# Two FFN layers' entries and ends re-ordered, and the attention's 16-row value blocks padded to 128 rows

## The chip, the cores and the metric

The kernel runs on one core of a Trainium2 chip. The core has five engines that run at the same time and wait for one another only where data passes: TensorE (PE, matmuls), VectorE (DVE), ScalarE (ACT), GpSimd (POOL) and SyncE (SP, which issues the DMAs here). The metric is the device time of one execution in microseconds. Times of one execution are also given per engine from a profile.

## The reference, cut to what matters

Two layers over 1040 tokens (16 meta tokens ahead of 1024), width 1024. Each layer mixes attention and convolution, and then runs a SwiGLU FFN of width 2816:

```python
h = jnp.concatenate([meta, x], axis=1)                 # 16 + 1024 tokens
for l in range(2):
    hn = rmsnorm(h, norm1_g[l])
    q, k, v, u = jnp.split(hn @ w_in[l], ...)
    attn_out = diff_attention(q, k, v, lam, ...)       # a = p0 - lam*p1;  a @ v; causal, 4 heads
    conv_out = conformer_conv(u + b_glu[l], ...)       # width 31, layer norm, silu
    h = h + jnp.concatenate([attn_out, conv_out], axis=-1) @ w_out[l]
    hn = rmsnorm(h, norm2_g[l])
    gate, up = jnp.split(hn @ w_gate_up[l], 2, axis=-1)
    h = h + (jax.nn.silu(gate) * up) @ w_down[l]
return rmsnorm(h, final_g)[:, 16:]
```

All is float32. The kernel writes most products as three matmuls on a high and a low part of each operand (high*high, high*low, low*high).

## The kernel before

Activations lie transposed, channels on the 128 partitions and tokens along the free dimension. The 1040 tokens go in chunks `CH0` = 272, 384 and 384 (in the last layer `CH1`, 2 x 512, since the meta tokens are dropped). A layer has two phases, each with a tile pool of its own that is opened at its start and closed at its end.

**The mix phase.** For each head: `project_qk`, `project_v`, `attention`, woven together with the projections of the next head so that TensorE always has work. In `attention`, the 1040 keys are cut into nine blocks, the first of 16 (the meta tokens) and eight of 128. `turn` transposes the softmaxed rows of one query block into `aT` (128 keys by 128 queries) and, for the meta keys, into `aT0`, 16 rows by 128. `values` then sums over the key blocks in one PSUM tile: one matmul on 16 rows (`aT0` and `v0`) and then one on 128 rows for each further block (L482). A float32 matmul is two records in the trace.

After the heads come the convolution and the output projection `w_out`. Its attention half ("oa") runs beside the convolution's layer norm (`conv_norm`, which calls `rsqrt_bcast`), its convolution half ("oc") in a loop of its own at L861: eight output blocks n in the order `OCN` = 0, 4, 1, 5, 2, 6, 3, 7, each in three (last layer: two) chunks of 12 matmuls into a PSUM tile "pj", added into `acc[n]` (the tiles ST and p) by DVE. After each pair (k, k+4), `forms(k)` makes the seven operand forms of a Strassen-Winograd product ("a11", "s3", "s2", "a12", "s1", "a22", "s4") from `acc[k]` and `acc[k+4]`, each split into a high part (ACT) and a low part (DVE), and `squares` adds the squares of both for the norm ahead of the FFN.

**The FFN phase.** 22 blocks j of 128 FFN channels. For each, seven products, in the order `PRODS`, of 2 x 12 matmuls of 260 columns (last layer 12 of 512), on PSUM tiles "pj", "tr" and "sc". The weights of a product are combined and split by `prep`, called two products ahead through `ahead`. The product "s1" adds into the same PSUM tiles ("sc") as "s2"; between them ACT copies the tiles out (L943), and before the change "a12" stands between the two. The norm factor `rs` is worked out in block j = 0 at "s3" by `rsqrt_bcast`: matmuls with a column of ones (L179), a power on POOL (L186), a diagonal on DVE (L197), a broadcast by matmuls with ones (L198), a copy by ACT (L201). The finished blocks (`mids`, high and low part) are gathered in groups of `GROUPS` = 3, 3, 3, 3, 3, 3, 2, 2, and `down` multiplies a group by `w_down` and adds it into `acc`, at "s3" of the next block. Of the last group nothing is left to overlap with: in layer 0 it also makes the next layer's operands (L281 and L282) and squares, in layer 1 the final norm, chunk by chunk (`CHF`, 512, 256 and 256 tokens), with the output multiplications at L914 and the DMAs of the output.

**What sets the order.** A list scheduler sorts the instructions of each engine; waits between engines are semaphores. PSUM tags have 3 tiles ("pj"), 3 ("sc") and 2 ("tr"). The pool of big tiles "S" has 15, the pool "T" of temporaries 5, and the weight slots "w" 16.

## Time and profile before

| | us |
|---|---|
| median of three runs | 2444.1 (2441.98 to 2445.82) |
| the profiled execution, its own time | 2446.08 |
| its span, first to last instruction | 2444.3 |
| PE busy | 2369.1 (97%) |
| DVE busy | 1689.7 (69%) |
| ACT busy | 991.1 (41%) |
| POOL busy | 32.4 (1%) |

The span lies 1.8 us under the execution's own time. The mean granted clock of TensorE is 0.985. In the chain of work that ended last PE has 82%, DVE 12%, ACT 2%. The stages follow one another: mix of layer 0 to 467 us, its oc loop to 530, FFN of layer 0 to 1239, mix of layer 1 to about 1685, its oc loop to 1733, FFN of layer 1 to 2391.8, and the last group with the final norm to the end.

### The profile page before, as it was taken

What the parts mean: (1) busy time and instruction counts of PE and PEld (TensorE: products, weight loads), DVE (VectorE), ACT (ScalarE), POOL (GpSimd) and SP (SyncE); (2) the same over time, 40 slices, a digit from 0 to 9 for tenths busy, and PEclk for the clock granted to TensorE, in tenths of its full rate; (3) what the DMA queues carried; (4) which work ended last, traced back from release to release, by engine and by line L of the source; (5) the groups of instructions that cost most, each with busy time, mean ns of one, the idle gap of its engine ahead of it and who ended that gap; (6) DMA issues with size and microseconds to landing.
All of it is one profiled execution on the core that took longest, in us unless ns stands there. A gap on an engine that the chain in (4) does not pass through costs nothing.

```text
span 2444.3 us, 36772 instructions
## 1 busy us (share of the span) xinstructions
PE 2369.1 (97%) x14359; PEld 2154.2 (88%) x14359; DVE 1689.7 (69%) x3532; ACT 991.1 (41%) x2090; POOL 32.4 (1%) x21
## 2 busy tenths in 40 slices
PE   8999999989999999999999999999999999999996
PEld 7889999889999999999989999987788888888885
DVE  7676799776656656566776767997866556556566
ACT  5554462544224224233435545635533223223232
POOL 0000000000000000000000000000000000000000
PEclk9999999999999999999989999999999999999998
DMA  4322412101111111111144224221111111111112
GB/s 163 87 67 73 118 60 63 39 27 52 50 57 49 48 57 46 55 47 48 56 130 104 72 58 118 70 62 39 35 57 46 54 57 46 54 56 46 55 50 71
DMA packets 86764, 155.28 MB, mean 64 GB/s; under 512 B 10304, under 2 KB 37952, under 8 KB 86592
## 3 DMA queue, kind: packets, MB, share of 16 engines
q1 hardware_dynamic: 86592, 152.95, 21.6%
q8 instruction: 113, 1.85, 0.3%
q14 instruction: 59, 0.48, 0.1%
HBM read 114.64 MB, written 8.45 MB: 50 GB/s over the span
## 4 chain that ended last, share of the span: by engine, by line
PE 82%; DVE 12%; ACT 2%; issue 1%; POOL 1%; DMA 1%; SPq 1%; DVEq 0%; POOLq 0%; ACTq 0%
PE pj L271 25%; PE sc L856 15%; PE pj L856 10%; PE tr L856 10%; PE sc L271 9%; PE tr L482 4%; DVE S L569 3%; PE sc L434 2%; PE tr L471 1%; PE sc L435 1%; DVE S L158 1%; PE sc L198 1%; DVE T L285 1%; DVE S L285 1%; PE sc L179 1%
## 5 line engine op out<-in xcount | busy, mean ns | idle before, releaser
L271 PE MATMUL pj<-S,w 128*128 128x384 f32 (+2 forms) x1425 | 358.2, 357 | 16.9 <-DVE ST L285 13.4
L271 PE MATMUL pj<-hh,w 128*128 128x384 f32 (+1 forms) x1776 | 348.5, 331 | 3.1 <-ACT w L221 2.4
L277 ACT ACTIVATE w<-w 128x512 fp32r<-128x512 f32 x308 | 187.2, 627 | 309.8 <-DVE w L285 129.5
L271 PEld LDWEIGHTS pj<-hh,w 128*128 128x128 f32 x1776 | 290.6, 192 | 6.0 <-ACT w L221 2.7
L271 PEld LDWEIGHTS pj<-S,w 128*128 128x128 f32 x1425 | 254.6, 192 | 45.6 <-DVE ST L285 15.2
L856 PE MATMUL sc<-S,w 128*128 128x260 f32 (+1 forms) x1188 | 283.9, 320 | 0.0
L278 DVE TENSOR_TENSOR w<-w,w 128x512 fp32r<-128x512 f32 x308 | 210.1, 688 | 95.5 <-ACT w L277 35.9
L221 ACT ACTIVATE w<-w 128x512 fp32r<-128x512 f32 (+2 forms) x219 | 121.0, 553 | 284.3 <-DMA w<-in_w_down 265.1
L271 PE MATMUL sc<-m,w 128*128 128x384 f32 (+3 forms) x834 | 229.8, 349 | 0.0
L271 PE MATMUL pj<-m,w 128*128 128x384 f32 (+3 forms) x825 | 226.9, 349 | 0.0
L856 PEld LDWEIGHTS sc<-S,w 128*128 128x128 f32 x1188 | 196.3, 188 | 17.4
L222 DVE TENSOR_TENSOR w<-w,w 128x512 fp32r<-128x512 f32 (+2 forms) x219 | 130.9, 598 | 92.4 <-ACT w L221 47.0
L856 PE MATMUL sc<-hh,w 128*128 128x260 f32 (+1 forms) x594 | 189.8, 320 | 0.7 <-ACT sc L932 0.7
L856 PE MATMUL sc<-hl,w 128*128 128x260 f32 (+1 forms) x594 | 189.8, 319 | 0.0
L271 PE MATMUL pj<-hl,w 128*128 128x384 f32 (+1 forms) x888 | 175.9, 329 | 0.0
L271 PE MATMUL sc<-S,w 128*128 128x384 f32 (+3 forms) x474 | 164.6, 349 | 6.3 <-DVE ST L285 2.7
L271 PEld LDWEIGHTS sc<-m,w 128*128 128x128 f32 x834 | 150.7, 188 | 14.1
L271 PEld LDWEIGHTS pj<-m,w 128*128 128x128 f32 x825 | 148.7, 188 | 13.8
L856 PE MATMUL pj<-hh,w 128*128 128x260 f32 (+1 forms) x594 | 157.8, 320 | 1.1 <-DVE ST L285 1.1
L856 PE MATMUL tr<-S,w 128*128 128x260 f32 (+1 forms) x594 | 158.1, 320 | 0.1
L856 PE MATMUL tr<-hl,w 128*128 128x260 f32 (+1 forms) x594 | 158.1, 320 | 0.0
L856 PE MATMUL pj<-S,w 128*128 128x260 f32 (+1 forms) x594 | 157.8, 320 | 0.0
(199 smaller groups left out, 4495.8 us busy)
## 6 DMA issues: line engine op xcount, KB each, us to landing
w<-in_w_gu SPq DMA_DIRECT2D x176, 256.0 KB, 2.8
S<-ST SPq DMA_DIRECT2D x96, 260.0 KB, 5.3
w<-in_w_in SPq DMA_DIRECT2D x80, 256.0 KB, 3.2
w<-in_w_down SPq DMA_DIRECT2D x96, 192.0 KB, 2.4
w<-in_w_out SPq DMA_DIRECT2D x32, 256.0 KB, 2.7
S<-in_xT SPq DMA_DIRECT2D x8, 520.0 KB, 7.1
w<-in_w_down SPq DMA_DIRECT2D x32, 128.0 KB, 2.0
S<-in_tabs SPq DMA_DIRECT2D x4, 520.0 KB, 5.2
```

The source lines that it names most:

```text
L158: V.tensor_tensor(sqacc[:, c0:c1], sqacc[:, c0:c1], q[:, :c1 - c0], op=ALU.add)
L179: T_.matmul(pst[:b - a, i:i + 1], lhsT=t[:, a:b], rhs=ones[:, 0:1], start=(q == 0), stop=(q == len(sq) - 1))
L221: S.activation(hi, rw, AF.Copy)
L222: V.tensor_tensor(lo, rw, hi.bitcast(F32), op=ALU.subtract)
L271: T_.matmul(out, lhsT=w[k][wi], rhs=xs[k][xi][:, c0:c1], start=(q == 0 and k == 0), stop=(q == 2 and k == n - 1))
L277: S.activation(hi, src, AF.Copy)
L278: V.tensor_tensor(lo, src, hi.bitcast(F32), op=ALU.subtract)
L285: V.tensor_tensor(o, a, b, op=op)
L434: T_.matmul(pc[:sz, :n], lhsT=qs[:, qa:qb], rhs=kk[:, k0:k1], start=True, stop=False)
L482: T_.matmul(po[:sz, :P], lhsT=lh, rhs=rh, start=(j == 0), stop=(j == len(blocks) - 1))
L569: bg.append(lambda o=o: V.scalar_tensor_tensor(y[:, o:L], z[:, :L - o], cw(o), y[:, o:L], op0=ALU.mult, op1=ALU.add))
L856: T_.matmul(outs[c][:, :s1 - s0], lhsT=w[wi][:, k * P:(k + 1) * P], rhs=xc[q][k][xi][:, s0:s1], start=(first and p == 0 and k == 0), stop= ...
```

## The change

1. **Padding.** `make_pads`, at the opening of each mix phase, makes four tiles of 128 x 128 and sets them to zero on POOL. `v0` and `aT0` become the first 16 rows of such a tile (two of each, in turn), and the first matmul of `values` takes all 128 rows, 112 of them zero.
2. **The norm in two parts.** `rsqrt_bcast` becomes `rsqrt_cols` (sums and power) and `spread` (diagonal, broadcast, copy). In the FFN the first is called at "s2" of block 0 and the second at "s1"; `conv_norm` yields between them.
3. **Forms in pieces.** `forms(k)` becomes a generator of four pieces, whose high and low parts are interleaved across forms; a piece is taken after each chunk of the oc loop (`some(1)`). The oc chunks alternate between PSUM "pj" and "tr". The first weights of the FFN (`ahead(1)`) are prepared after the oc loop instead of ahead of it, and the squares of the last four output blocks are done inside block 0.
4. **Order of products.** "s1" now follows "s2" at once, ahead of "a12".
5. **Groups.** The groups are 3, 3, 3, 3, 3, 3, 4. The fourth block's result takes two S tiles. In the last group four outputs run over the first three blocks before the fourth is there (`early`). In layer 1 the closing of a chunk (norm and output) is written after the second output block of the next chunk (`owed`).

The core of the diff:

```diff
-GROUPS = ((3, 3, 3, 3, 3, 3, 2, 2), (3, 3, 3, 3, 3, 3, 2, 2))
+GROUPS = ((3, 3, 3, 3, 3, 3, 4), (3, 3, 3, 3, 3, 3, 4))
-PRODS = ("a11", "s3", "s2", "a12", "s1", "a22", "s4")
+PRODS = ("a11", "s3", "s2", "s1", "a12", "a22", "s4")
...
-                    plan.append((("dn", l, gi, n), (w_down[l, n, :, f0:f0 + gn, :], gn), end and n < 5))
+                    plan.append((("dn", l, gi, n), (w_down[l, n, :, f0:f0 + gn, :], gn), end and n >= 4))
...
+    def make_pads():
+        pads[:] = [[phase[1].tile([P, P], F32, tag=f"pad{i}{j}", name=nm("pad")) for j in range(2)]
+                   for i in range(2)]
+        for t in pads[0] + pads[1]:
+            G.memset(t, 0.0)
...
-        v0 = phase[1].tile([META, P], F32, tag="v0", name=nm("v0"), bufs=2)
+        v0 = padded(0)
...
-                S.activation(v0, px[:META, :P], AF.Copy, scale=rcol[:META, 0:1])
+                S.activation(v0[:META, :], px[:META, :P], AF.Copy, scale=rcol[:META, 0:1])
...
-                    aT0 = phase[1].tile([META, P], F32, tag="aT0", name=nm("aT0"), bufs=2)
-                    S.activation(aT0[:, :sz], ptg[:META, 384:384 + sz], AF.Copy)
+                    aT0 = padded(1)
+                    S.activation(aT0[:META, :sz], ptg[:META, 384:384 + sz], AF.Copy)
...
             S.activation(s4, y[:, b0:b1], AF.Copy, scale=e)
+            hi("a11")
+            tt(d, x[:, b0:b1], x[:, a0:a1], ALU.subtract)
             stt(s3, x[:, b0:b1], g, s4, ALU.subtract)
...
+            lo("a11")
+            hi("s3")
+            yield
             stt(s2, d, g, s4, ALU.subtract)
...
-        ahead(1)
...
+        no = 0
         for i, n in enumerate(OCN):
             w = fetch("oc", l, n)
             t = acc[n]
             for c0, c1 in chunks:
-                po = ps("pj")
+                po = ps(("pj", "tr")[no % 2])
+                no += 1
                 mm3(po[:, :c1 - c0], w, ccats, c0, c1)
                 tt(t[:, c0:c1], po[:, :c1 - c0], t[:, c0:c1], ALU.add)
+                some(1)
             if i % 2:
-                forms(n - 4)
-                squares(n - 4)
-                squares(n)
+                todo.append(forms(n - 4))
+                if i < 5:
+                    todo += [squares(n - 4), squares(n)]
+        ahead(1)
+        some(99)
+        todo += [squares(n) for n in OCN[4:]]
...
+            early = 4 if end else 0
+            pos = []
+            for n, (c0, c1) in outs[:early]:
...
+                mm3_some(po[:, :c1 - c0], ws[n], mids, c0, c1, range(gn - 1), True, False)
+            for (n, (c0, c1)), po in zip(outs, pos):
+                mm3_some(po[:, :c1 - c0], ws[n], mids, c0, c1, [gn - 1], False, True)
+                settle(n, c0, c1, po)
...
+                if end and last:
+                    if owed and n == 2:
+                        close(owed.pop())
+                    if n == KD - 1:
+                        owed.append((c0, c1))
+            for c in owed:
+                close(c)
...
+                if j == 0:
+                    some(2)
+                    bl = range(1 if last else 0, NQ)
+                    if q == "s2":
+                        some(99)
+                        rc = rsqrt_cols(sqacc, D, bl)
+                    if q == "s1":
+                        rs = spread(rc, bl)
...
                 if q == "s3":
-                    if j == 0:
-                        rs = rsqrt_bcast(sqacc, D, range(1 if last else 0, NQ))
```

How the change moves instructions is shown at three places. The first is DVE in layer 0's oc loop, around the forms of the second pair (k = 1); T are temporaries, hh and hl homes of forms, S_5071 or S_5039 the sum of squares, ST and p the accumulators, and a row with "pj" or "tr" as its input adds one oc chunk and so frees that PSUM tile. Before:

```order
807 L768 TENSOR_TENSOR hl_92<-T_5317,hl_92 128x520
808 L768 TENSOR_TENSOR hl_87<-T_5316,hl_87 128x520
809 L777 SCALAR_TENSOR_TENSOR T_5315<-T_5318,par,T_5317 128x520
810 L282 SCALAR_TENSOR_TENSOR hl_90<-T_5318,par,hl_90 128x520
811 L777 SCALAR_TENSOR_TENSOR T_5314<-p_4444,par,T_5315 128x520
812 L768 TENSOR_TENSOR hl_88<-T_5315,hl_88 128x520
813 L158 TENSOR_TENSOR S_5071<-S_5071,T_5338 128x520
814 L768 TENSOR_TENSOR hl_91<-T_5314,hl_91 128x520
815 L158 TENSOR_TENSOR S_5071<-S_5071,T_5341 128x520
816 L158 TENSOR_TENSOR S_5071<-S_5071,T_5344 128x520
817 L158 TENSOR_TENSOR S_5071<-S_5071,T_5347 128x520
818 L285 TENSOR_TENSOR ST_4442<-pj_5356,ST_4442 128x272
```

And now:

```order
803 L293 TENSOR_TENSOR ST_4410<-pj_5270,ST_4410 128x272
804 L293 TENSOR_TENSOR T_5288<-ST_4409 128x520
805 L793 SCALAR_TENSOR_TENSOR T_5286<-ST_4409,par,T_5287 128x520
806 L793 SCALAR_TENSOR_TENSOR T_5285<-T_5288,par,T_5287 128x520
807 L293 TENSOR_TENSOR ST_4410<-tr_5295,ST_4410 128x384
808 L793 SCALAR_TENSOR_TENSOR T_5284<-p_4412,par,T_5285 128x520
809 L293 TENSOR_TENSOR hl_87<-T_5286,hl_87 128x520
810 L293 TENSOR_TENSOR ST_4410<-pj_5314,ST_4410 128x384
811 L293 TENSOR_TENSOR hl_89<-T_5285,hl_89 128x520
812 L793 SCALAR_TENSOR_TENSOR hl_88<-T_5288,par,hl_88 128x520
813 L293 TENSOR_TENSOR p_4413<-tr_5338,p_4413 128x272
```

The rows that free PSUM stood behind a block of fourteen or more form and square rows; now one stands behind every second or third row.

The second place is DVE behind the oc loop, where the weights of the FFN's first products are made (rows that write a w tile; the last accumulation of the loop is row 839 now). Before, the weights of "s2" (rows 825, 827, 828) and "a12" (row 830) stand inside the loop, among the accumulations of its sixth output block:

```order
825 L285 TENSOR_TENSOR w_5630<-w_5074,w_5076 128x512
826 L285 TENSOR_TENSOR p_4445<-pj_5418,p_4445 128x384
827 L285 TENSOR_TENSOR w_5631<-w_5072,w_5630 128x512
828 L278 TENSOR_TENSOR w_5635<-w_5631,w_5634 128x512
829 L285 TENSOR_TENSOR p_4445<-pj_5432,p_4445 128x384
830 L278 TENSOR_TENSOR w_5667<-w_5078,w_5666 128x512
831 L285 TENSOR_TENSOR ST_4442<-pj_5493,ST_4442 128x272
```

Now the weights of "a11" and "s3" stand right behind the loop, those of "s2" (rows 854, 856, 859) behind the forms of the last pair, and squares among and behind them:

```order
848 L793 SCALAR_TENSOR_TENSOR T_5533<-p_4414,par,T_5534 128x520
849 L293 TENSOR_TENSOR S_5549<-T_5534,S_5549 128x520
850 L793 SCALAR_TENSOR_TENSOR S_5547<-T_5537,par,S_5547 128x520
851 L793 SCALAR_TENSOR_TENSOR S_5553<-p_4414,par,S_5553 128x520
852 L293 TENSOR_TENSOR S_5555<-T_5533,S_5555 128x520
853 L293 TENSOR_TENSOR S_5559<-T_5536,S_5559 128x520
854 L293 TENSOR_TENSOR w_5574<-w_5517,w_5519 128x512
855 L158 TENSOR_TENSOR S_5039<-S_5039,T_5610 128x520
856 L293 TENSOR_TENSOR w_5575<-w_5515,w_5574 128x512
857 L158 TENSOR_TENSOR S_5039<-S_5039,T_5613 128x520
858 L158 TENSOR_TENSOR S_5039<-S_5039,T_5616 128x520
859 L286 TENSOR_TENSOR w_5579<-w_5575,w_5578 128x512
```

So the making of weights moved from inside the loop to behind it.

The third place is DVE in layer 1's last group, around the norm of the second chunk, the first of 256 tokens. S_23532 or S_23206 is the sum of squares, rows of L182, L197 or L179, L198 are the norm, rows of L914 or L971 multiply the output, and rows that read "sc" or "pj" and write ST or p add an output block of the last chunk. Before:

```order
3181 L158 TENSOR_TENSOR S_23532<-S_23532,T_23786 128x256
3182 L182 TENSOR_SCALAR s_23790<-sc_23789 128x2
3183 L175 MEMSET s_23907 128x16
3184 L197 TENSOR_SCALAR T_23798<-con,s_23795 128x128 x2
3185 L914 SCALAR_TENSOR_TENSOR ST_17663<-ST_17663,par,S_23533 128x256 x2
3186 L914 SCALAR_TENSOR_TENSOR ST_17664<-ST_17664,par,S_23533 128x256 x2
3187 L914 SCALAR_TENSOR_TENSOR p_17665<-p_17665,par,S_23533 128x256
3188 L914 SCALAR_TENSOR_TENSOR p_17666<-p_17666,par,S_23533 128x256
3189 L914 SCALAR_TENSOR_TENSOR p_17667<-p_17667,par,S_23533 128x256
3190 L914 SCALAR_TENSOR_TENSOR p_17668<-p_17668,par,S_23533 128x256
3191 L285 TENSOR_TENSOR ST_17663<-sc_23829,ST_17663 128x256
3192 L285 TENSOR_TENSOR ST_17664<-sc_23851,ST_17664 128x256
```

And now:

```order
3121 L293 TENSOR_TENSOR ST_17507<-pj_23554,ST_17507 128x256
3122 L158 TENSOR_TENSOR S_23206<-S_23206,T_23517 128x256
3123 L293 TENSOR_TENSOR ST_17507<-sc_23569,ST_17507 128x256
3124 L158 TENSOR_TENSOR S_23206<-S_23206,T_23534 128x256
3125 L158 TENSOR_TENSOR S_23206<-S_23206,T_23551 128x256
3126 L158 TENSOR_TENSOR S_23206<-S_23206,T_23583 128x256
3127 L293 TENSOR_TENSOR ST_17508<-pj_23586,ST_17508 128x256
3128 L179 TENSOR_SCALAR s_23604<-sc_23603 128x2
3129 L174 MEMSET s_23720 128x16
3130 L198 TENSOR_SCALAR T_23612<-con,s_23609 128x128
3131 L158 TENSOR_TENSOR S_23206<-S_23206,T_23600 128x256
3132 L198 TENSOR_SCALAR T_23612<-con,s_23609 128x128
```

Before, the accumulations that read "sc" (row 3191 on) stood behind all eight output multiplications; now those of the last chunk's first three output blocks, "sc" included, stand ahead of the norm, and the rest behind the multiplications.

## Rows read from the trace of the kernel before

**Rows 1.** Stretches: PE, PEld, DVE, ACT, POOL busy us (instructions), PEclk, DMA share, GB/s.
```profile
70.00:280.00 210.00, 208.29 (x1328) 189.27 (x1329) 143.00 (x499) 112.82 (x336) 4.74 (x3) 0.98 0.28 71
280.00:375.00 95.00, 92.84 (x601) 86.30 (x600) 87.78 (x208) 51.40 (x124) 4.33 (x2) 1.00 0.32 90
467.00:531.00 64.00, 52.53 (x306) 51.68 (x305) 50.52 (x85) 28.93 (x50) 0.00 (x0) 0.92 0.10 30
1208.70:1239.20 30.50, 24.23 (x146) 22.73 (x144) 30.03 (x67) 21.20 (x47) 0.00 (x0) 0.97 0.38 141
1240.00:1250.00 10.00, 10.00 (x44) 9.55 (x43) 5.63 (x12) 3.83 (x8) 0.00 (x0) 0.50 0.79 278
1685.00:1733.00 48.00, 45.64 (x188) 36.37 (x189) 40.93 (x66) 25.65 (x44) 0.00 (x0) 0.96 0.09 28
2369.40:2391.80 22.40, 22.40 (x98) 18.14 (x98) 13.00 (x22) 7.82 (x15) 0.00 (x0) 1.00 0.16 48
2391.80:2430.00 38.20, 29.34 (x169) 25.61 (x167) 31.27 (x73) 12.07 (x29) 1.70 (x2) 0.87 0.22 79
```

**Rows 2.** Timeline of PE in layer 0's attention: start, duration, line, tiles, count.
```profile
261.50 0.32 PE L435 MATMUL sc<-S,S 128*128 128x348 f32 x1
261.75 0.48 PE L482 MATMUL tr<-v,aT 16*128 16x128 f32 x2
262.16 0.49 PE L482 MATMUL tr<-S,aT 128*128 128x128 f32 x2
...
262.65 0.32 PE L435 MATMUL sc<-S,S 128*128 128x346 f32 x1
...
262.96 0.32 PE L435 MATMUL sc<-S,S 128*128 128x346 f32 x1
263.12 1.05 PE L482 MATMUL tr<-S,aT 128*128 128x128 f32 x8
263.93 0.41 PE L434 MATMUL sc<-S,S 128*128 128x348 f32 x1
264.18 0.32 PE L435 MATMUL sc<-S,S 128*128 128x348 f32 x1
```

**Rows 3.** Line L482 by form: ns min/median/max, first and last start us.
```profile
L482 PE MATMUL tr<-v,aT x136: 268/278/416, 76.0 to 1577.7; 16*128 16x128 f32 x128, 16*16 16x128 f32 x8
```

**Rows 4.** Timeline of PE in layer 0's oc loop, idle time before and its releaser.
```profile
488.30 11.61 PE L271 MATMUL pj<-S,w 128*128 128x272 f32 x72 [2.93 <-DVE ST L285]
...
504.36 15.83 PE L271 MATMUL pj<-S,w 128*128 128x272 f32 x84 [4.21 <-DVE ST L285]
...
524.50 5.80 PE L271 MATMUL pj<-S,w 128*128 128x384 f32 x24 [4.07 <-DVE ST L285]
```

**Rows 5.** Timeline of DVE in the same loop.
```profile
502.05 1.91 DVE L158 TENSOR_TENSOR S<-S,T 128x520 f32<-128x520 f32 x3
503.88 1.36 DVE L285 TENSOR_TENSOR ST<-pj,ST 128x272 f32<-128x272 f32 x3
...
508.45 0.68 DVE L285 TENSOR_TENSOR w<-w,w 128x512 f32<-128x512 f32 x1
```

**Rows 6.** The chain that ended last, one product of layer 0's FFN.
```profile
553.50 2.87 PE sc L856 x24
```

**Rows 7.** Timeline of PE behind layer 0's last group.
```profile
1239.25 3.84 PE L271 MATMUL pj<-hh,w 128*128 128x272 f32 x12 [2.37 <-ACT w L221]
```

**Rows 8.** Timeline of all engines in the last chunk of the final norm.
```profile
2429.67 0.28 PE L271 MATMUL sc<-m,w 128*128 128x256 f32 x1
...
2433.45 1.02 PE L179 MATMUL sc<-ones,S 128*128 128x1 f32 x4 [3.50 <-DVE S L158]
```

**Rows 9.** Line L943, ACT's copy of product "s2", by form.
```profile
L943 ACT ACTIVATE T<-sc x66: 365/388/602, 547.8 to 2381.0; 128x260 f32<-128x260 f32 x44, 128x512 f32<-128x512 f32 x22
```

**Rows 10.** POOL's groups: busy us, mean ns.
```profile
L186 POOL TENSOR_TENSOR s<-s,mhalf 128x9 f32<-128x9 f32 (+3 forms) x9 | 14.6, 1621 | 1751.0 <-DVE s L184 982.3 <-DVE s L182 754.6 <-DVE s L175 14.1
L1080 POOL MEMSET const-float32-0.0<- 128x1 f32 x1 | 0.1, 98 | 0.2 <-issue 0.2
```

More of the change, by code (lines that the diff above doesn't have):

```diff
@@ L186, in rsqrt_bcast, with spread @@
         G.tensor_tensor(rc[:, i0:i1], ms[:, i0:i1], mhalf[:, i0:i1], op=ALU.pow)
+        return rc
+    def spread(rc, blocks=range(NQ), out=None):
         r = big() if out is None else out
@@ L272, in mm3, with mm3_some @@
                           start=(q == 0 and k == 0), stop=(q == 2 and k == n - 1))
+    def mm3_some(out, w, xs, c0, c1, ks, first, last):
+        for k in ks:
+            for q, (wi, xi) in enumerate(((0, 0), (0, 1), (1, 0))):
+                T_.matmul(out, lhsT=w[k][wi], rhs=xs[k][xi][:, c0:c1],
+                          start=(first and q == 0 and k == ks[0]), stop=(last and q == 2 and k == ks[-1]))
     hs = list(zip(hh, hl))
@@ L892, in down, with settle @@
                 order = [(n, chunks) for n in range(KD)]
-            for n, cs in order:
+            def settle(n, c0, c1, po):
+                t = acc[n]
+                tt(t[:, c0:c1], po[:, :c1 - c0], t[:, c0:c1], ALU.add)
+                if end:
+                    if not last:
+                        gsplit(hh[n][:, c0:c1], hl[n][:, c0:c1], t[:, c0:c1], col("g1", l + 1, n))
+                    accum_sq(sq[0], n == 0, t[:, c0:c1], c0, c1)
+            outs = [(n, c) for n, cs in order for c in cs]
@@ L907, in down @@
[L907 to L916 removed]
+                    mm3(po[:, :c1 - c0], ws[n], mids, c0, c1)
@@ L918, in build @@
+                    settle(n, c0, c1, po)
+                if end and not last and c1 == L:
+                    nc.sync.dma_start(hsave[n], acc[n])
+                if end and last:
[5 more added lines that the diff above has]
+                close(c)
         f0 = gi = 0
```

117 lines of the change are left out of this document (71 added, 46 removed).

## The prediction

> **What bounds the kernel now.** I read the page first: PE is busy for 97% of the span, so the whole is a chain of matmuls, and a gain is either less PE time or less idle and half-clock time of PE. Then the stretches [rows 1], to find where PE is not full. In the attention of heads 0 to 2 it is busy for 208.29 of 210.00 us and DVE for 143.00, so PE alone sets the pace; beside head 3 DVE has 87.78 of 95.00. In layer 0's oc loop PE has only 52.53 of 64.00 at a clock of 0.92; the last group of layer 0 is DVE's (30.03 of 30.50, PE 24.23), and the ten microseconds from 1240 run at a clock of 0.50, the 1.2 GHz level, with PE full. Layer 1's oc loop has 2.36 us of idle time, its end (2391.8 to 2430) 8.9 at a clock of 0.87, and the last 14.3 us hold almost no matmul. Last come the timelines of these places, for what PE waits for there: accumulations by DVE (L285), three times in the oc loop [rows 4], with square and form rows ahead of them in DVE's queue [rows 5]; a weight split behind layer 0's last group [rows 7]; the sum of squares before the final norm [rows 8].
>
> **Padding.** The change adds rows of zeros and no instruction on PE. In rows 2, from the L435 ahead of the 16-row block to the next L435 behind L434 it takes 262.65 - 261.50 = 1.15 us, with four L482 records between. The same stretch with 128-row records alone would be 263.12 - 262.96 = 0.16 into them, four at (263.93 - 263.12) / 8 = 0.10, and 264.18 - 263.93 = 0.25 out: 0.82. So 0.33 us hang on the 16-row block. The same difference by start times of like pairs, over all 68 blocks (136 records, [rows 3]), has a median of 0.38. The ceiling is 68 x 0.38 = 26 us. 51 blocks lie beside heads 0 to 2 of the two layers, where PE is full: of 19.4 us I take nine tenths, 17.5. Of the 17 beside head 3 (6.5 us), where DVE is nearly full, half, 3.2. Sum **20.7**; bounds 0 (if the time is not the sixteen rows') and 26. The trace shows extra time at both borders of the block and within it, not that it is the number of rows that causes it. POOL's eight memsets have no row of their size: between 0.1 us and a power's 1.6 [rows 10] each, on an engine that is 1% busy; layer 1's four wait for the tiles of layer 0's FFN and stand ahead of the norm's power there. If they end late, that power waits, and behind it the projection's DVE rows: 0 to 6 us. I take 0, since the last down products free those tiles well before the power.
>
> The Trainium skill bears on this from two sides. "TensorEngine Tiling (Array Packing)", section Key Properties, says that a change of the tiling mode drains TensorE; by that the block's borders cost and the padding takes them away. "TensorE: Matmul & The Clock Gate", section "Why this matters for your kernels", says that a single matmul on 32 rows takes as long as one on 128; by that alone the padding would give nothing, and the sum would be 20.7 us less. The trace agrees with the first as far as a stretch with the block is longer.
>
> **Layer 0's oc loop and entry.** The loop's matmuls are eight blocks like those in rows 4: 72 in 11.61 us, so 5.8 for a block's 36, 46.4 in all; the loop took 63 (467.2 to 530.1). The difference is 2.93 + 4.21 + 4.07 = 11.2 of waiting and, after waits, matmuls at half clock: 15.83 against 84/72 x 11.61 = 13.5, and 5.80 against 4.2 (24 x 0.174), together about 4. Now the accumulations stand among the forms (first order fence), on two PSUM tags; of DVE's 50.52 us in the stretch [rows 1] some 11.5 move behind the loop (below), and 39 fit under 46.4. So about 16 are removed. Against it: the weights of "s2" now stand behind the loop's last forms (second fence). From the last accumulation to the low part of "s2" DVE has seventeen rows of 0.6 to 0.7 us, about 11.5. PE has only "a11" and "s3" meanwhile, 2 x 2.87 [rows 6], and starts them about 1.5 late: some 4 to 5 us idle, partly paid again at half clock (1 to 2), and squares and power end later, another 1 to 2. Sum 16 - 7.5 = **+8.5**, bounds 2 and 15.
>
> **Layer 1's.** The same chain, but there was little to win: 2.4 us idle and about 1.4 of half clock in the loop [rows 1]. 3.8 - 5.8 = **-2**, bounds -5 and +2.
>
> **Layer 0's end.** Two groups of two blocks become one of four. The group that ran beside DVE work takes 22.8 us of pure PE; the last took 30.5 and the wait of 2.37 [rows 1, 7] is in it: 53.3 together. Four blocks are 45.5 of PE (eight times the 36 matmuls of rows 4). DVE's part falls under that: it had 30.03 for the same eight outputs with their low parts and squares, and with the low parts of twice the weights (eight rows more of 0.7, as the w row in rows 5) it has 36; the other group's accumulations are gone. Gain 7.8. At the same time the cause of the half clock behind it goes: ten microseconds at 0.50 [rows 1] and parts of the five on either side are 6 to 7 us of lost work in the next layer's first projection. **14**, bounds 6 (clock still low) and 16.
>
> **Layer 1's end.** Before: 22.4 for the group beside "s3" [rows 1] and 52.5 from 2391.8 to the end of the span, 74.9. After: 44.8 of matmuls (twice 22.4); norms of two chunks on PE, 3.2; about 1 of waits; from the last matmul to the end 12.3 (before 14.3 from 2429.95, of which 3.5 wait for squares [rows 8]; fewer stand in the queue now). 61.3, gain **13.6**, bounds 9 and 15.
>
> **Order of the products.** "s1" adds into the tiles that ACT must first copy for "s2". The copy takes 0.39 in the median, 0.60 at most [rows 9]. Before, the whole "a12", 2.87 us, covered it; now, in layer 0, it is the other half of the same product, 1.44 [rows 6], and in layer 1 four matmuls of "a12" that the order puts between, 0.93. Measured from the end of "s2" the 66 copies were over after at most 0.50 in layer 0 and 0.86 in layer 1. Covered by little: **-1.5** for some late ones, bounds 0 and -12. The norm in two parts costs no instruction; its rows are off the path except in block 0, where they are in the entry's sum.
>
> **Sum.** 20.7 + 8.5 - 2 + 14 + 13.6 - 1.5 = 53.3. Against the profiled execution, 2446.08, that gives 2392.8; its span is 2444.3, the rest lies around it and stays. Against the median, 2 us lower, 2390.8. I say **2392**.
>
> **Rivals.** (1) *The padding gives nothing*, either because a matmul that starts a sum costs this whatever its rows, or because PE then waits for ACT's copies of the transposed blocks instead. For it: the records after the 16-row ones are slow too [rows 2]. Against: later 128-row blocks between the same L434 are not. 2392 + 20.7 = 2413. (2) *The entries wait more than they save*: "s2" weights, squares and power come one after another behind the loop, PE idles three times and its clock falls for ten microseconds behind it. Then layer 0 gives -3 instead of 8.5, and layer 1 -7: 2392 + 16.5 = 2408. For it: the second order fence; against: ACT and DVE are otherwise free there. (3) *The hand-over of "s2" to "s1" stalls each block*, the side on which it is slower. In each of the 44 blocks "s1" waits when ACT stands in a weight copy of 0.63 and one of its other copies as the product ends. One in front: 0.63 + 0.39 - 0.93 is 0.1 in layer 1, nothing in layer 0; three in front, 2.3 - 1.2 = 1.1 a block, 48 us. From 1.25 us a block (55 us) the whole gain is gone, with the half clock that repeated waits bring, 1.5 a block gives 2392 + 65 = 2457. Against it: ACT is busy for 41%, and the copies ended within 0.9 us so far. (4) *The fourth block comes late*: its S tiles and the last weights wait for operands to be free, and both ends gain only half: 2392 + 14 = 2406.
>
> **Chances.** The forecast as it stands (2382 to 2400) 0.50, (1) 0.14, (2) 0.12, (4) 0.10, (3) in a mild form (2400 to 2425) 0.06 and to its end 0.05, two of the first three rivals together 0.03. The range takes in the sum's bounds that go together and the single rivals: 2378 to 2420; outside lie (3) to its end, two rivals together and some of the mild (3), about 0.1, and as much for what is not thought of. 0.2%, 5 us, is what a measurement of this kernel can tell from no change. Faster 0.90, same 0.04 (what of (3) and of two rivals together falls there), slower 0.06.
>
> **What would show it.** In the profile after: L482 with 128 rows only, and the like stretch 0.8 us long; the attention stretches 8 to 11 us shorter in each layer. The oc loop of layer 0 in 46 to 49 us with no wait over 1, then a wait for the "s2" weights of 4 to 5 us before its first matmul. PE full from the last "s4" of layer 0 to the next layer, at full clock there. 60 to 62 us from the last group's begin to the end. No wait at "s1" in the steady blocks, 20.1 us each in layer 0. The prediction is wrong if the attention keeps its length, or if the steady blocks of the FFN grow.

## The result and the profile after the change

| | before | after |
|---|---|---|
| median, us | 2444.96 (4 runs, 2441.98 to 2446.26) | 2388.03 (4 runs, 2387.03 to 2388.52) |
| ratio | 1 | 0.9768, 95% interval 0.9751 to 0.9785 |
| profiled execution, its time and its span | 2446.08, 2444.3 | 2387.03, 2385.3 |
| PE busy | 2369.1 | 2333.7 (98% of its span) |
| DVE busy | 1689.7 | 1670.9 |
| mean granted clock of TensorE | 0.985 | 0.992 |

The change takes 57 us off. 2392 was forecast, with 2378 to 2420 around it. The two spans differ by 59.0 us. Cut at the same instructions in both traces (start times, worked out from the traces), they divide like this (from the convolution norm's first matmul to FFN block 1 is called a layer's entry below):

| from, to | before | after | difference | forecast |
|---|---|---|---|---|
| start to the first score matmul of layer 0 | 62.4 | 62.0 | -0.4 | 0 |
| first to last score matmul, layer 0 | 285.4 | 274.5 | -11.0 | -20.7 |
| the same, layer 1 | 278.1 | 268.4 | -9.6 | (both layers) |
| last score to the convolution norm's first matmul, both layers | 138.1 | 137.6 | -0.5 | 0 |
| convolution norm to FFN block 1, layer 0 | 139.7 | 130.1 | -9.6 | -8.5 |
| the same, layer 1 | 127.6 | 126.8 | -0.8 | +2 |
| FFN block 1 of layer 0 to the first score matmul of layer 1 | 729.2 | 714.4 | -14.8 | -14 |
| FFN block 1 of layer 1 to the end | 683.8 | 671.5 | -12.3 | -13.6 |

The order of the products, +1.5 in the forecast, lies in the last four rows. The steady FFN blocks are 20.13 us long instead of 20.11 in layer 0 and 19.51 instead of 19.47 in layer 1, which is 1.2 us over all of them.

The stretches of the kernel after that answer to [rows 1] (columns: PE, PEld, DVE, ACT and POOL busy us with instructions, granted clock, DMA share, GB/s). The first is layer 0's oc loop, the second and third what follows it, then layer 0's last group of four blocks with the clock behind it, layer 1's oc loop from its fifth microsecond on with the first products behind it, and the last two cover layer 1's last group and the end:

```profile
452.00:500.00 48.00, 47.83 (x301) 47.34 (x300) 43.54 (x75) 26.07 (x43) 0.00 (x0) 1.00 0.13 39
...
506.00:520.00 14.00, 9.46 (x67) 9.09 (x66) 12.28 (x23) 10.74 (x22) 0.00 (x0) 0.88 0.14 48
520.00:530.00 10.00, 10.00 (x67) 9.46 (x67) 6.21 (x20) 2.57 (x6) 2.18 (x1) 0.83 0.01 2
1163.70:1209.00 45.30, 45.30 (x288) 45.30 (x287) 38.24 (x78) 27.48 (x58) 0.36 (x3) 1.00 0.39 135
...
1220.00:1230.00 10.00, 10.00 (x62) 10.00 (x60) 6.96 (x18) 1.55 (x4) 0.00 (x0) 1.00 0.01 2
...
1640.00:1690.00 50.00, 47.24 (x200) 38.09 (x199) 45.84 (x74) 29.39 (x50) 0.00 (x0) 0.97 0.16 50
...
2323.70:2372.00 48.30, 47.59 (x306) 42.76 (x306) 33.71 (x74) 13.56 (x29) 1.71 (x2) 1.00 0.17 61
2372.00:2385.30 13.30, 2.72 (x16) 2.13 (x14) 6.42 (x18) 1.82 (x6) 0.70 (x1) 0.68 0.30 100
```

Layer 0's oc loop is full (47.83 of 48.00, where [rows 1] has 52.53 of 64.00). Right behind it is the price: 9.46 of 14.00, and a clock of 0.88 and 0.83 up to 530. The last group of layer 0 is PE's, 45.30 of 45.30, DVE has 38.24 of them, and the clock behind it stays at 1.00, the 2.4 GHz level.

The timeline of PE at the like place in the attention as [rows 2]:

```profile
252.51 0.32 PE L456 MATMUL sc<-S,S 128*128 128x348 f32 x1
252.67 0.38 PE L503 MATMUL tr<-pad,pad 128*128 128x128 f32 x2
252.89 0.39 PE L503 MATMUL tr<-S,aT 128*128 128x128 f32 x2
...
253.27 0.32 PE L456 MATMUL sc<-S,S 128*128 128x346 f32 x1
```

253.27 - 252.51 = 0.76, where [rows 2] has 1.15. And the timeline of PE behind layer 0's oc loop; in brackets the idle time ahead of a row and what ended it:

```profile
503.28 0.39 PE L901 MATMUL tr<-hh,w 128*128 128x260 f32 x1 [0.66 <-ACT w L285]
...
504.57 0.39 PE L901 MATMUL tr<-S,w 128*128 128x260 f32 x1 [0.31 <-ACT S L802]
...
512.71 0.39 PE L901 MATMUL sc<-hh,w 128*128 128x260 f32 x1 [4.54 <-ACT w L285]
```

This is the wait for the weights of "s2" that was forecast as 4 to 5 us.

### The profile page after: what moved, and what is told of

Its sections match the earlier page's. It is cut to its first block, busy times and chain, and to the rows that moved or that the text cites. A ratio compares the mean times of both kernels' runs of the same rounds, so it can differ in the third digit from the quotient of the medians.

```text
span 2385.3 us, 36659 instructions
## 1 busy us (share of the span) xinstructions
PE 2333.7 (98%) x14407; PEld 2140.8 (90%) x14407; DVE 1670.9 (70%) x3476; ACT 987.2 (41%) x2074; POOL 33.8 (1%) x29
## 4 chain that ended last, share of the span: by engine, by line
PE 86%; DVE 9%; ACT 2%; issue 1%; POOL 1%; DMA 1%; SPq 1%; DVEq 0%; POOLq 0%; ACTq 0%
PE pj L272 26%; PE sc L901 16%; PE pj L901 10%; PE tr L901 10%; PE sc L272 10%; DVE S L590 4%; PE tr L503 3%; PE tr L272 2%; PE sc L455 2%; PE tr L492 1%; PE sc L456 1%; PE sc L199 1%; DVE S L293 1%; DVE cw L610 1%; DVE S L286 1%
## 5 line engine op out<-in xcount | busy, mean ns | idle before, releaser
L272 PE MATMUL pj<-hh,w 128*128 128x384 f32 (+1 forms) x1776 | 342.5, 327 | 0.7 <-ACT S L368 0.7
L272 PE MATMUL pj<-S,w 128*128 128x384 f32 (+3 forms) x1164 | 296.2, 351 | 1.5 <-ACT S L285 0.9
L222 ACT ACTIVATE w<-w 128x512 fp32r<-128x512 f32 (+1 forms) x204 | 117.6, 577 | 308.3 <-DMA w<-in_w_down 167.9
L272 PEld LDWEIGHTS pj<-S,w 128*128 128x128 f32 x1164 | 204.4, 188 | 22.8 <-ACT S L285 1.9
L272 PE MATMUL sc<-m,w 128*128 128x384 f32 (+3 forms) x804 | 211.5, 346 | 0.0
L272 PE MATMUL pj<-m,w 128*128 128x384 f32 (+3 forms) x804 | 211.4, 346 | 0.0
L223 DVE TENSOR_TENSOR w<-w,w 128x512 fp32r<-128x512 f32 (+1 forms) x204 | 127.1, 623 | 51.7 <-ACT w L222 45.2
L272 PEld LDWEIGHTS sc<-m,w 128*128 128x128 f32 x804 | 143.1, 188 | 12.7
L272 PEld LDWEIGHTS pj<-m,w 128*128 128x128 f32 x804 | 143.1, 188 | 12.6
L590 DVE SCALAR_TENSOR_TENSOR S<-S,par,S 128x1037 f32<-128x1037 f32 (+15 forms) x120 | 153.2, 1278 | 0.6
```

The source lines that it names most:

```text
L222: S.activation(hi, rw, AF.Copy)
L223: V.tensor_tensor(lo, rw, hi.bitcast(F32), op=ALU.subtract)
L272: T_.matmul(out, lhsT=w[k][wi], rhs=xs[k][xi][:, c0:c1], start=(q == 0 and k == 0), stop=(q == 2 and k == n - 1))
L590: bg.append(lambda o=o: V.scalar_tensor_tensor(y[:, o:L], z[:, :L - o], cw(o), y[:, o:L], op0=ALU.mult, op1=ALU.add))
```

## The experiments

The experiments were measured in four sets (1 to 4, 5 to 8, 9 to 11, and 12), each beside the kernel before, whose medians were 2443.7, 2444.0, 2447.1 and 2444.5. The small differences are therefore read from the traces, cut at the same instructions as in the table above. A trace is one execution: in experiments 1, 2 and 5 PE, DVE, ACT and POOL have the same order in the entries as in the changed kernel, and still layer 0's entry is 129.1, 130.7 and 130.1 us long (130.1 in the changed kernel) and layer 1's 127.6, 127.7 and 128.5 (126.8). A difference of up to 1 us in layer 0's entry, or of up to 1.7 us in layer 1's, is thus not told from nothing.

**1. Sixteen rows again.** The padded tiles stay, the first matmul of a sum reads only their first 16 rows.

```diff
-                    blocks.append((aT0[:, :sz], v0))
+                    blocks.append((aT0[:META, :sz], v0[:META, :]))
```

> The changed kernel, but the first matmul of each sum over the values takes only the 16 rows again (the padded tiles and their memsets stay, so nothing moves on any engine). Theory (the number of rows costs the time): 68 blocks x 0.38 = 26 us at most, 20.6 as the attention stretches of the two traces differ; so 2388.0 + 20.6 = 2408.6, between 2406 and 2414, and in the trace the like stretch of PE is 0.33 to 0.38 us longer at each block. Rival (a matmul that starts a sum costs it, whatever its rows, and the attention became shorter by something else): 2388, within 2.

Measured: 2406.98 us, 19.0 over the changed kernel; the two attention stretches are 285.6 and 277.2 us, 11.1 and 8.8 longer. The same place as above, on PE:

```profile
261.79 0.32 PE L456 MATMUL sc<-S,S 128*128 128x348 f32 x1
262.03 0.48 PE L503 MATMUL tr<-pad,pad 16*128 16x128 f32 x2
262.45 0.49 PE L503 MATMUL tr<-S,aT 128*128 128x128 f32 x2
...
262.93 0.32 PE L456 MATMUL sc<-S,S 128*128 128x346 f32 x1
```

1.14 us again instead of 0.76. No instruction moved on any engine, so the number of rows is the cause; the rival, a cost of starting a sum, falls, and so does a wait for the copies of the transposed blocks, which are the same here.

**2. Sixty-four rows.**

```diff
-                    blocks.append((aT0[:, :sz], v0))
+                    blocks.append((aT0[:64, :sz], v0[:64, :]))
```

> The same with 64 rows instead of 16 or 128 (48 of them zero). If every matmul on fewer than 128 rows among those on 128 pays (a change of the array's shape), 2408 as with 16 rows. If only the small ones pay, or the cost falls with the rows missing, 2388, or halfway, about 2398 (48 of 112 rows filled would give 2400). I take 2408.

Measured: 2406.72 us, the same as with 16 rows; at the same place 261.18 - 260.03 = 1.15:

```profile
260.03 0.32 PE L456 MATMUL sc<-S,S 128*128 128x348 f32 x1
260.28 0.48 PE L503 MATMUL tr<-pad,pad 64*128 64x128 f32 x2
...
261.18 0.32 PE L456 MATMUL sc<-S,S 128*128 128x346 f32 x1
```

Four times the rows changed nothing. It is not a price by rows missing: 16 and 64 rows cost the same between matmuls on 128, and 128 cost no more than any other block. Where the time lies is shown by PE's weight loads (PEld), in the changed kernel and here:

```profile
252.51 0.35 PEld L503 LDWEIGHTS tr<-pad,pad 128*128 128x128 f32 x2
252.78 0.30 PEld L503 LDWEIGHTS tr<-S,aT 128*128 128x128 f32 x2
```

```profile
260.27 0.29 PEld L503 LDWEIGHTS tr<-pad,pad 64*128 64x128 f32 x2 [0.22 <-issue]
260.69 0.30 PEld L503 LDWEIGHTS tr<-S,aT 128*128 128x128 f32 x2
```

On 128 rows the load starts while an earlier matmul runs, 0.16 and 0.11 us ahead of its own matmul (252.67 and 252.89). On 64 rows, and again on the 128 rows behind them, the first load starts together with its own matmul (260.28 and 260.69); with 16 and with 64 rows this is so at all 68 blocks. The four gaps between matmul starts around a block are about 0.1 us longer each (medians), 0.38 together. The Trainium skill, "TensorEngine Tiling (Array Packing)", section Key Properties, says that changing the tiling mode drains TensorE; both traces agree with it as far as no load is taken ahead at either change of rows. What the sizes between 64 and 128 do was not tried.

**3. The first weights inside the loop.** The first three products' weights are prepared ahead of the seventh output block.

```diff
             w = fetch("oc", l, n)
+            if i == 6:
+                ahead(2)
             t = acc[n]
...
-        ahead(1)
         some(99)
```

> The changed kernel, with the weights of the FFN's first three products prepared ahead of the seventh output block of the oc loop instead of behind the loop. The 4.54 us that PE waits for the s2 weights in layer 0 and the 2.39 in layer 1 were put down to their standing behind the last forms on DVE. Theory: both waits go, and what of the norm comes next stays (squares and power, 1 to 2 us each), the half clock behind them goes too: 5 to 9 us less, 2379 to 2383. Rival (the forms and squares of the last pair are what is late, whatever the weights): the products wait for a later operand instead, 2386 to 2389. Other side: the weight rows in the loop delay the accumulations again, 2390 or more, with PE waits on DVE inside the loop.

Measured: 2386.94 us, 1.1 less. The trace: layer 0's entry 126.75 instead of 130.1, layer 1's 127.1 instead of 126.8; in the profiled execution the first score matmul came 2.0 us later. In layer 0 the 4.54 us wait went, and smaller ones came:

```profile
506.71 0.39 PE L901 MATMUL tr<-hh,w 128*128 128x260 f32 x1 [1.49 <-DVE p L293]
...
516.19 0.39 PE L901 MATMUL pj<-hh,w 128*128 128x260 f32 x1 [0.78 <-ACT w L285]
```

Of the two theories each holds in one layer. In layer 0 the weights were late and the place of their preparation is worth 3.4 us. In layer 1 the rival holds: there the wait of 2.39 us for the weights goes too, but PE now waits 2.22 and 2.13 us for the high parts of the last pair's forms (ACT, L802; one such wait of 2.75 in the changed kernel) and 0.98 for a copy, and nothing is gained. The expectation had both layers gain.

**4. Two groups of two again.**

```diff
-GROUPS = ((3, 3, 3, 3, 3, 3, 4), (3, 3, 3, 3, 3, 3, 4))
+GROUPS = ((3, 3, 3, 3, 3, 3, 2, 2), (3, 3, 3, 3, 3, 3, 2, 2))
```

> The changed kernel with the last group of four blocks cut into two of two again, in both layers (first outputs over one block early, and the deferred closing of a chunk, stay). Theory (the gain at both ends is the work of two groups under one last group's DVE rows): 13.5 + 13.2 = 26.7 us back, 2414.7; with part of it due to the early outputs and the deferred closing, at least half back, 2402 to 2416. Rival (early outputs and deferred closing are what helped): 2388 to 2395.

Measured: 2415.71 us, 27.7 more. From FFN block 1 to the next layer's scores 729.4 us (729.2 before the change), from block 1 of layer 1 to the end 683.1 (683.8). Layer 0's end has the rows of before back, the last wait of 2.37 [rows 7] and the half clock among them (stretch, then PE's timeline):

```profile
1187.90:1218.50 30.60, 24.36 (x147) 22.53 (x145) 30.07 (x67) 20.85 (x46) 0.64 (x4) 0.96 0.38 141
...
1220.00:1230.00 10.00, 10.00 (x45) 9.55 (x44) 5.01 (x13) 3.63 (x8) 0.00 (x0) 0.50 0.76 265
```

```profile
1214.83 0.39 PE L272 MATMUL sc<-S,w 128*128 128x272 f32 x1 [1.79 <-DVE w L223]
...
1218.41 3.83 PE L272 MATMUL pj<-hh,w 128*128 128x272 f32 x12 [2.37 <-ACT w L222]
```

So the group of four carries what both ends gained; the early outputs and the deferred closing bring nothing without it.

**5. No early outputs.**

```diff
-            early = 4 if end else 0
+            early = 0
```

> The changed kernel without the four early outputs: in the last group of four each output runs over all four blocks at once. Theory (a group of four alone has enough matmuls to cover DVE, but its first output then waits for the fourth block's products): the fourth block needs DVE and ACT rows of about 3 us behind its last product, which the early outputs cover now; so 2 to 4 us a layer, 4 to 8 in all, 2392 to 2396, with one PE wait of 2 to 3.5 us at the first down matmul of each last group and some half clock behind it. Rival (other matmuls stand ahead anyway, or the scheduler orders them alike): 2388, within 1.5.

Measured: 2388.63 us, and 2386.5 of span. No wait above 0.3 us stands ahead of a down matmul of either last group: without the early outputs the scheduler itself puts matmuls of the next outputs ahead of the fourth block's. The theory falls; the part is worth nothing that can be measured.

**6. Closing a chunk at once.**

```diff
-                    if owed and n == 2:
-                        close(owed.pop())
                     if n == KD - 1:
-                        owed.append((c0, c1))
-            for c in owed:
-                close(c)
+                        close((c0, c1))
```

> The changed kernel, with each chunk of the final norm closed at once behind its last output block, as before the change, instead of behind the second block of the next chunk. Theory: PE waits at the norm's column sums for the last squares and again for the power, 2 to 4 us for each of the first two chunks (3.91 and 1.42 stood there before, rows of the kernel before), 4 to 8 in all with half clock: 2392 to 2396. Rival (the group of four alone has removed those waits, since DVE is no longer behind): 2388 to 2389.

Measured: 2388.48 us. PE waits 0.79 for the first chunk's norm (0.57 with the deferred closing) and nowhere else before the last chunk; the end is 0.6 us longer. The theory falls here too. With DVE no longer behind, nothing is late that the deferral would cover. The early outputs and the deferral were not left out together.

**7. The old order of the products.** In block 0 the first half's gate uses the mix phase's norm factor, since the FFN's is written later.

```diff
-PRODS = ("a11", "s3", "s2", "s1", "a12", "a22", "s4")
+PRODS = ("a11", "s3", "s2", "a12", "s1", "a22", "s4")
```

> The changed kernel with the products in the old order (s2, a12, s1). In the steady blocks the two orders differ by 0.02 us in layer 0 and 0.04 in layer 1 (20.11 against 20.13 and 19.47 against 19.51), 1.3 us in all, which would come back. In block 0 the norm is written at s2 and s1 and its factor is first needed by a12, which then follows s2 at once: theory, a12's evacuation waits for the norm and with it the PSUM tiles, 1 to 4 us in each layer. Sum: 2388 to 2394. Rival (the order matters nowhere): 2386.7.

Measured: 2386.70 us, 1.3 less. Steady blocks 20.16 us in layer 0 (20.13) and 19.49 in layer 1 (19.51): the order is worth next to nothing there, and no PE wait stands at "s1" in the changed kernel's. The entries, in which block 0 here waits for no norm, are 1.8 us shorter in layer 0 and 3.6 in layer 1. But in layer 1 the convolution norm's first matmul, where the entry begins, came 2.5 us later than in the changed kernel (71.55 against 69.02 us behind the last score). From the last score to block 1 only 1.4 and 1.0 us are gained, hardly more than such stretches vary by. So the norm costs that at most here, and not the 3.5 us that the expectation of experiment 9 counts for layer 1.

**8. Forms in one piece.** The loop as before in three things.

```diff
+        ahead(1)
         no = 0
...
-                po = ps(("pj", "tr")[no % 2])
+                po = ps("pj")
...
-                some(1)
...
+                some(99)
-        ahead(1)
         some(99)
```

> The changed kernel with the oc loop as before in three things: the forms of a pair come in one piece behind it, its outputs use PSUM pj alone, and the first weights stand ahead of the loop (the last pair's squares stay in block 0, and the norm in its two parts). Theory (the block of form rows ahead of the accumulations made PE wait three times): the loop of layer 0 has waits of 3 to 4 us on DVE again, 7 to 11 in all, and half clock behind two of them, while the wait for the s2 weights goes: from the convolution's end to the second FFN block 135 to 140 us against 130.1, layer 1 within 1.5 of 126.8; so 2393 to 2398. Rival (what shortened the entry is the squares of the last pair and the norm in two parts): 2386 to 2390.

Measured: 2393.86 us, 5.8 more; the entries are 133.3 (130.1) and 128.7 (126.8). The three waits of [rows 4] are back, each somewhat shorter:

```profile
477.46 11.62 PE L272 MATMUL pj<-S,w 128*128 128x272 f32 x72 [2.40 <-DVE ST L293]
...
492.92 13.15 PE L272 MATMUL pj<-S,w 128*128 128x272 f32 x72 [3.60 <-DVE ST L293]
...
508.79 5.94 PE L272 MATMUL pj<-S,w 128*128 128x272 f32 x36 [2.47 <-DVE ST L293]
```

Layer 0's loop takes 58.5 us (46.0 in the changed kernel, 63.1 before), and what follows it to block 1 takes 25.1 (34.4, and 25.9 before). The three things together (pieces, second PSUM tag, place of the weights; they were not taken apart) save 12.5 in the loop and pay 9.3 behind it. Net 3.1 in layer 0, under what was expected (135 to 140 for the entry), and 1.95 in layer 1, a little over it; the sum is in the expected range. The rest of layer 0's gain, 6.4, is there without the three, so part of the rival holds as well. Layer 1's 1.95 is hardly more than what its entry varies by.

**9. The old order, with the whole norm at "s2".**

```diff
-PRODS = ("a11", "s3", "s2", "s1", "a12", "a22", "s4")
+PRODS = ("a11", "s3", "s2", "a12", "s1", "a22", "s4")
...
-                    if q == "s1":
-                        rs = spread(rc, bl)
+                        rs = spread(rc, bl)
```

> The changed kernel with the products in the old order (s2, a12, s1) and the whole norm written at s2 of block 0, so that a12 finds its factor. The kernel with the old order alone took a12's factor of block 0 from another norm; its steady blocks (20.16 and 19.49 us against 20.13 and 19.51) showed that the order matters nowhere there, and its block 0, which waited for no norm, was 1.8 us shorter in layer 0 and 3.5 in layer 1. Theory (the new order is for block 0, where s1 gives the norm 2.9 us more): from the convolution's end to the second block 131 to 134 us in layer 0 (130.1 in the changed kernel) and 128 to 131 in layer 1 (126.8), 2390 to 2395. Rival (PSUM lets the evacuation of a12 be late, nothing on PE waits for the factor): 2388, within 1.5.

Measured: 2390.36 us, a ratio to the kernel before of 0.9768, the same as the changed kernel's. In the trace the entries are 131.8 and 127.2, 1.7 and 0.4 longer. Layer 0's lies in the expected range, layer 1's does not, and its 0.4 is not told from nothing. The steady blocks are shorter again, 20.12 us in layer 0 and 19.47 in layer 1 (20.13 and 19.51 in the changed kernel), about 1 us over all of them. So the new order is worth some 2 us in block 0 at most and costs about half of that in the other blocks; the times can't tell the sum from nothing.

**10. All squares ahead of block 0.**

```diff
-                if i < 5:
-                    todo += [squares(n - 4), squares(n)]
+                todo += [squares(n - 4), squares(n)]
...
-        todo += [squares(n) for n in OCN[4:]]
```

> The changed kernel with the squares of the last four output blocks written behind the forms of their pair, before block 0, instead of inside block 0. Theory (they are eight DVE rows of 0.61 us that stand ahead of the weights of s2 then): the wait for the s2 weights grows from 4.5 to 6 or 8 us in layer 0, and the norm ends earlier by little; 2389 to 2394, half of it in each layer. Rival (the scheduler puts them by their readiness, wherever they are written): 2388, within 1.5.

Measured: 2395.71 us, a ratio of 0.9789 (0.9768 for the changed kernel), about 5 us more; the intervals of the two ratios overlap, but in its own set it is 5.4 us above experiment 9 (2390.36), with no run of one among the other's. The entries are 131.8 and 130.8, 1.7 and 4.0 longer. PE's waits behind layer 0's loop:

```profile
506.42 0.39 PE L901 MATMUL tr<-hh,w 128*128 128x260 f32 x1 [2.60 <-ACT w L285]
...
515.21 2.08 PE L177 MATMUL sc<-ones,S 128*16 128x1 f32 x18 [2.44 <-DVE S L158]
...
518.81 0.58 PE L901 MATMUL sc<-hh,w 128*128 128x260 f32 x1 [1.52 <-ACT w L285]
```

The wait stands at "s3" and the norm's column sums now, not where it was expected, but the size is right and the rival falls: where the squares are written decides what DVE does first. Deferring them is worth about 5 us, most of it in layer 1 (4.0, well over what that entry varies by).

**11. Squares summed on POOL too.** For each of the last four outputs DVE adds the first half of the tokens and POOL the second, beside the weights of experiment 3 in layer 0.

```diff
+            if i == 6 and not last:
+                ahead(2)
...
-        todo += [squares(n) for n in OCN[4:]]
+        todo += [squares_late(n) for n in OCN[4:]]
...
+        def squares_late(n):
+            q = phase[1].tile([P, L], F32, tag="m", name=nm("q"), bufs=4)
+            for x, (c0, c1) in enumerate(half):
+                S.activation(q[:, c0:c1], acc[n][:, c0:c1], AF.Square)
+                (V, G)[x].tensor_tensor(sqacc[:, c0:c1], sqacc[:, c0:c1], q[:, c0:c1], op=ALU.add)
+            yield
```

> A version meant to be faster than both: the changed kernel with the weights of the first three products prepared ahead of the seventh oc block in layer 0 (in layer 0 that shortened the entry by 3.4 us), and in both layers the squares of the last four output blocks summed half by DVE and half by POOL, which does nothing there. Theory (the norm ends late because DVE sums eight rows, 5 us, just before it): layer 0 from 130.1 to 124 to 126, layer 1 from 126.8 to 124 to 126; 2380 to 2384. Rival (POOL's adds take 1.2 us or more each and end after DVE's eight would have, or slow DVE beside them): 2384 to 2390.

Measured: 2394.48 us, a ratio of 0.9785, 4.1 us above experiment 9 of the same set. The entries are 132.5 and 130.7, 2.4 and 3.9 longer than the changed kernel's. Two of POOL's eight adds, and DVE's rows at the same time:

```profile
502.51 1.56 POOL L846 TENSOR_TENSOR S<-S,q 128x520 f32<-128x520 f32 x1 [7.34 <-ACT q L845]
509.90 1.61 POOL L846 TENSOR_TENSOR S<-S,q 128x520 f32<-128x520 f32 x1 [5.83 <-ACT q L845]
```

```profile
502.82 1.81 DVE L793 SCALAR_TENSOR_TENSOR S<-T,par,S 128x520 fp32r<-128x520 f32 x1
504.55 0.68 DVE L286 TENSOR_TENSOR w<-w,w 128x512 fp32r<-128x512 f32 x1
...
510.28 1.79 DVE L793 SCALAR_TENSOR_TENSOR T<-T,par,T 128x520 f32<-128x520 f32 x1
```

A row of this form on DVE takes 0.75 us elsewhere. Here it takes 1.8, and it ends 0.56 us after POOL's add does, both times. The same stands at all eight: each add takes 1.3 to 2.6 us on POOL instead of 0.69, and a DVE row with two operands in SBUF ends 0.55 or 0.56 us behind it, 0.4 to 1.1 us late. The rival's second half holds. Which of PE's waits come from it is argued only: behind layer 0's loop PE waits 1.91 and 2.19 us for DVE's accumulations and 1.96 for the norm's diagonal, in layer 1 2.08 and 3.71 for high parts of forms, where the changed kernel has one such wait of 2.75.

**12. The version to hand on.** Experiment 3 in layer 0 alone.

```diff
             w = fetch("oc", l, n)
+            if i == 6 and not last:
+                ahead(2)
             t = acc[n]
```

> The version to be handed on: the changed kernel with the weights of the first three products prepared ahead of the seventh oc block in layer 0 alone (in both layers it shortened layer 0's entry by 3.4 us and lengthened layer 1's by 0.35). Theory: layer 0's entry is 126.8 us again, layer 1's 126.8; 3.4 us less than the changed kernel, 2384 to 2386, a ratio to the kernel before of 0.975 to 0.976. Rival (the 3.4 are a matter of one execution): 2387 to 2389, and 129 or more for the entry in the trace.

Measured: 2385.77 us (5 runs, 2383.89 to 2386.82), a ratio to the kernel before of 0.9754, interval 0.9741 to 0.9768; 2.3 less than the changed kernel. Layer 0's entry is 126.7 us, layer 1's 126.8, as expected. It is the fastest of the kernels that compute the whole, but the intervals of the two ratios overlap, so the times alone do not show the 2.3 us. The 3.4 us in layer 0's entry stand in two traces, 126.75 in experiment 3 and 126.7 here, outside of the 129.1 to 130.7 that executions with the weights behind the loop have.

## Why the prediction was right, point by point

**Padding, 20.7 forecast, 20.6 in the attention stretches and 19.0 when undone.** The step that was open, whether the number of rows is the cause, is shown by experiments 1 and 2. The conversion, nine tenths beside heads 0 to 2 and half beside head 3, was taken without a row, but it came out right in its parts as well. Since PE runs the same matmuls in the same order in experiments 1 and 2, the shift of their start times against the changed kernel tells where the time comes back: 16.5 and 14.9 us beside heads 0 to 2 of the two layers, where 17.5 were taken, and 3.5 in both beside head 3, where 3.2 were. POOL's memsets were put at 0 and are: layer 1's four take 0.64 us together, at 1208.64, and the power there starts at 1215.64 when DVE releases it (rows of POOL's timeline after):

```profile
1208.64 0.64 POOL L338 MEMSET pad<- 128x128 f32 x4 [686.37 <-PE sc L272]
1215.64 1.80 POOL L183 TENSOR_TENSOR s<-s,mhalf 128x9 f32<-128x9 f32 x1 [6.36 <-DVE s L442]
```

**Layer 0's entry, 8.5 forecast, 9.6 measured.** Its two terms were right nearly to the microsecond: the loop lost 17.1 us (63.1 to 46.0; 16 forecast), and what follows it gained 8.5 (25.9 to 34.4; 7.5 forecast), with the s2 weights' wait of 4.54 named ahead. The last 1.0 of the 9.6 lies ahead of the loop, where nothing was forecast (the convolution norm in two parts stands there; it was not taken back). What carries the gain is shown only in part. Taken back one by one, the pieces with their PSUM tag and the place of the weights are worth 3.1 (experiment 8), the deferred squares of the last pair 1.7 (experiment 10) and the order with the norm in two parts 1.7 (experiment 9). The rest stays open. The squares had no term of their own in the forecast; they came with the loop's shortening, as "of DVE's 50.52 us some 11.5 move behind the loop".

**Layer 1's entry, 2 us slower forecast, 0.8 faster measured.** "The same chain" behind the loop, 5.8, stood without a working of its own and was right: 27.3 us became 32.8, 5.5 more. The mis-sized term is the loop's 3.8. The loop went from 52.2 to 45.8 us, 6.4 less, and is 45.8 in experiments 1, 2 and 5 too. The forecast read its idle time from a stretch that begins at 1685, 4 us into the loop. The whole loop before, with two waits of PE that the stretch leaves out or cuts, and the whole loop after:

```profile
1681.00:1733.24 52.24, 48.22 (x197) 37.52 (x196) 45.07 (x71) 28.34 (x48) 0.00 (x0) 0.97 0.10 31
```

```profile
1683.12 1.42 PE L271 MATMUL pj<-S,w 128*128 128x512 f32 x4 [1.19 <-ACT S L277]
1685.19 18.09 PE L271 MATMUL pj<-S,w 128*128 128x512 f32 x77 [0.66 <-DVE S L278]
```

```profile
1635.15:1680.95 45.80, 45.07 (x194) 36.05 (x193) 41.37 (x64) 25.93 (x44) 0.00 (x0) 1.00 0.12 41
```

PE's idle time went from 4.0 us to 0.7, 3.3 instead of 2.4. Its busy time fell by 3.1 as the clock rose from 0.97 to 1.00, where 1.4 were put; a few FFN matmuls that stood in the loop of before are in that, and their share was not worked out.

**Layer 0's end, 14 forecast, 14.8 measured, with the clock back at 1.00.** Experiment 4 brings the old rows back in full. The 45.5 for four blocks is not what eight times the 36 matmuls of [rows 4] give, 46.4; the trace has 45.8, so little hangs on it. **Layer 1's end, 13.6 forecast, 12.3 measured**; 0.9 of the difference are the steady blocks.

**The order, 1.5 slower.** The steady blocks did grow by 0.02 and 0.04 us, 1.2 in all, which agrees in size, but not for the reason given: PE has no idle time above 0.03 us in these blocks, so it waits for no copy. The old order gives most of it back in experiment 9 (20.12 and 19.47) and not in experiment 7 (20.16 and 19.49), the grouping in two gives 19.49 in layer 1, and the scheduler orders each of these kernels a little differently. What makes the blocks longer stays open. "The prediction is wrong if the steady blocks of the FFN grow" was drawn too sharply: they grew by a quarter of a percent at most, where rival (3) has 1.1 us a block. The use of the new order for block 0's norm was not seen in the forecast; it is about 2 us.

**The rivals.** (1) fell by experiment 1. (2) was half right: in layer 1 PE waited three times behind the loop, 2.75, 2.39 and 0.66 us, in layer 0 once for long, 4.54 us, with the clock at 0.88 and 0.83 behind it, and in both layers the loop paid for it. (3) fell, no steady block waits at "s1". (4) fell: the first down matmul of each last group follows without a wait. What the forecast did not see is that two parts, the early outputs and the deferred closing, do nothing that can be measured (experiments 5 and 6); it had put each end in one sum and so could not tell its parts apart.

## What to carry to other kernels

When two operations on PE differ in the number of rows they contract, look at the start times around the odd one before its own duration: the matmul on 16 rows took 278 ns at the median, like its neighbours (275), and its place in the stream still cost 0.38 us; with zeros in the missing rows it did not. At a stage's border, count the work of the engine that feeds the next stage, not only the waits inside the loop: shortening the loop by 17 us laid 8.5 bare behind it, and 3.4 of those went when the weights stood earlier in DVE's queue. Where a last group has nothing left to overlap with, a larger one lets the matmuls cover its evacuation: one group of four blocks instead of two of two was worth 27 us here, and the finer re-orderings inside it were then worth nothing.

## What the runs showed of the hardware that was not expected

- Matmuls on 64 rows between matmuls on 128 cost what those on 16 rows do: 0.38 us for a block of two records, here some 19 us over 68 blocks. PE's matmul rows list no wait for it; it shows in the weight loads, which start 0.11 us or more ahead of their matmuls on 128 rows (medians) and not ahead at all where the number of rows changes.
- An add on POOL and a DVE row with two operands in SBUF do not run beside each other: DVE's row of 0.75 us took 1.81 and 1.79 while POOL's add took 1.56 and 1.61. DVE's rows that read one operand from PSUM kept their usual 0.43 and 0.69 us beside such adds (at 492.19 and 1677.58 of experiment 11). So two engines can hold each other up though no data passes between them. The Trainium skill, "SBUF — State Buffer", section "SBUF: two separate sides", says that the pair of ports that the two engines share is locked for a whole instruction, so that the other engine blocks; the trace agrees, DVE's row ends 0.56 us behind POOL's. Here an idle POOL was no free place for work that DVE does beside it.
